# Projection chunks that accumulate onto the running sum in PSUM, filled and copied back by ScalarE, and group-norm sums added onto zeros

## The chip, the cores and the metric

The kernel runs on one core of one Trainium2 chip. The core has a matrix engine (TensorE, PE in the profile) that writes into PSUM, eight banks of 128 partitions x 512 floats, a vector engine (VectorE, DVE), a scalar engine (ScalarE, ACT), GpSimd (POOL), and DMA queues that SyncE (SP), ScalarE and GpSimd issue to. The metric is the device time of one execution in microseconds, as the median of several runs. Each engine works through its own list of instructions in the order of that list, and waits for the others by semaphores.

## The reference, cut to what matters

One block of a diffusion backbone in float32: adaLN-modulated RMSNorm, one input projection, attention beside a short gated convolution, group norm, output projection, gated MLP. The change touches the input projection and the group norm of the convolution's half:

```python
h_l = modulate(rms_norm(x, g_mix_norm[l]), sh_a, sc_a)            # 512 tokens x 2048
qa_l, kva_l, kr_l, cb_l, cc_l, ch_l = split_projection(h_l @ w_in[l])
...
conv_l = short_conv(cb_l, cc_l, ch_l, conv_w[l], conv_b[l])
x = x + gt_a * merge_heads(att_l, conv_l, g_mix_out[l], w_out[l])  # RMSNorm over groups of 128, then @ w_out
```

## The kernel before

Everything is kept transposed: a tile is 128 features x 512 tokens. The input projection has 31 such output tiles ("columns" below, the weights in `ORDER`), and its sum runs over 16 input tiles h0 to h15. Float32 accuracy is made from a high and a low part of both operands: `mm3` (line 200) issues three matmuls for each product, high x high (L202), high x low (L203), low x high (L204). So each piece of weights is first cast by ScalarE (`split`, L181, the high part) and then subtracted by VectorE (L182, the low part).

The sixteen inputs become ready one after another, because each needs two rows of adaLN weights, which VectorE multiplies out (L256, and for the context L667) from `ada` tiles that stream in over SyncE's queue through four buffers. The projection is therefore cut into three chunks of the sum: `KCH = [2, 4, 10]` inputs. Chunk 0 (h0, h1) is written out earlier in the function. Chunks 1 and 2 run in the loop at lines 829 to 875. Each begins with six columns at once (`first_banks`, tiles `pf`, weights `wf` from loads `rf`), and goes on with the other 25 columns one by one: a bank from `bank`, tile `pp`, `n` calls of `mm3` (n = 4 in chunk 1, 10 in chunk 2), then `evac`. Weights come as `rw` loads: in chunk 1 four columns to a load on GpSimd's queue, in chunk 2 one column to a load of 640 KB on SyncE's queue. There are two raw buffers, and one is free again when VectorE has made its last low part; the cast weights (`w_0h`, `w_4h`, `w_8h` and the l's) have about five buffers.

`evac` (line 673) keeps a running sum `acc[m]` in SBUF. In chunk 0 ScalarE copies the bank there. In chunks 1 and 2 VectorE adds the bank to it (L678). After chunk 2 it starts what follows for the column: `low_rank`, `rope_key`, or, for the columns of the convolution, `conv` (L604 to L611), `gn_sum` and `gn_apply`. `gn_sum` (line 390) squares a finished tile on ScalarE (L392), sums it over the 128 features with four matmuls against a column of ones (L396), each into its own column of a bank, and lets VectorE copy the four numbers out (L397).

`bank` (line 120) deals banks in turn: four single ones (tag "s") and two double ones (tag "b"), whose halves go to two successive dealings, though both halves are one tile. So the columns 13 and 14 share the tile that the trace calls `pp_13`, 17 and 18 share `pp_17`, 21 and 22 share `pp_21`, and so on.

The order of the instructions on each engine is not written out by hand here, but where `keep` pins it: the framework's scheduler lays the program out on a timeline of its own and fixes the order by that. Loads through `fetch_to` are pinned to the program's order until chunk 1's first columns are done (`ordered`, L852), and are free after it.

Of the kernel before, what the change touches and what calls it, by code (L numbers as in the profile page):

```python
# [13 lines left out]
ALU = mybir.AluOpType  # L14
# [3 lines left out]
P = 128  # L18
# [57 lines left out]
def block_kernel(ctx, tc, xt, ctxt, ctxn, c, c_ctx, w_ada, small, w_in, w_inc, w_q, w_kv, w_out,  # L76
# [3 lines left out]
    V, A, G_, PE, SP = nc.vector, nc.scalar, nc.gpsimd, nc.tensor, nc.sync  # L80
# [19 lines left out]
    def t2(shape, dt, name):  # L100
        return act.tile(shape, dt, tag="t2", bufs=NT2, name=name)

    def tmp(shape, dt, name):
        return tp.tile(shape, dt, tag="tmp", bufs=5, name=name)
# [7 lines left out]
    def sml(nm):  # L112
        return one_bank[0](nm) if one_bank[0] else pp.tile([P, 512], F32, tag="s", bufs=4, name=nm)

    def big(nm):
        return pp.tile([P, 1024], F32, tag="b", bufs=2, name=nm)
# [3 lines left out]
    def bank(nm):  # L120

        if turn[1] is not None:
            h, turn[1] = turn[1], None
            return h
        i = turn[0] = (turn[0] + 1) % 6
        if i % 3:
            return sml(nm)
        b = big(nm)
        turn[1] = b[:, 512:]
        return b[:, :512]  # L130

    def first_banks(nm, n):
        turn[:] = (5 if n == 6 else 0), None
        r = [sml(f"{nm}{g}") for g in range(4)]
        for g in range(4, n, 2):
            b = big(f"{nm}{g}")
            r += [b[:, :512], b[:, 512:]]
        return r
# [55 lines left out]
    def part(w, i, n=1):  # L194
        return tuple(z[:, i * P:(i + n) * P] for z in w)
# [4 lines left out]
    def mm3(ps, w, x, first, last, on_top=False):  # L200
        with tc.issue_after(behind.pop()) if behind else ExitStack():
            PE.matmul(ps, w[0], x[0], start=first, stop=False, skip_group_check=on_top)  # L202
        PE.matmul(ps, w[0], x[1], start=False, stop=False, skip_group_check=on_top)  # L203
        PE.matmul(ps, w[1], x[0], start=False, stop=last, skip_group_check=on_top)  # L204
# [26 lines left out]
    ident, ones = io[:, :P], io[:, P:]  # L231
# [158 lines left out]
    def gn_sum(t, o):  # L390
        sq = tmp([P, T], F32, f"gq{t}")
        A.activation(sq, o, AF.Square)  # L392
        yield
        ps = sml(f"gp{t}")
        for g in range(4):
            PE.matmul(ps[:, g:g + 1], sq[:, g * P:(g + 1) * P], ones[:, 0:1], start=True, stop=True)  # L396
        V.tensor_copy(out=gn[:, 4 * t:4 * t + 4], in_=ps[:, :4])  # L397
        yield

    def gn_apply(t, o):  # L400
        pb = sml(f"gb{t}")
        spread(pb, gn[:, 4 * t:4 * t + 4])
        V.scalar_tensor_tensor(out=o, in0=o, scalar=s("g_out", 8 + t), in1=pb, op0=ALU.mult, op1=ALU.mult)
        yield
# [9 lines left out]
    def low_rank(tiles, g, width, nm, res):  # L414
        sq = None
        for t in tiles:
            sq = add_squares(sq, t, width, nm)
            yield
        r = tmp([P, T], F32, nm + "r")
        rms([sq], len(tiles) * P, width, r)  # L420
        yield
        for i, t in enumerate(tiles):
            V.scalar_tensor_tensor(out=t, in0=t, scalar=s(g, i), in1=r[:, :width], op0=ALU.mult, op1=ALU.mult)
            res.append(hilo(t, T, nm + f"{i}") if width == T else hilo_pair(t, nm + f"{i}"))
            yield
# [3 lines left out]
    with ExitStack() as pa:  # L429
# [19 lines left out]
        hl = {}  # L449
# [107 lines left out]
        for j in range(NK):  # L557
# [6 lines left out]
            if j in (2, 4, 6, 8):  # L564
                g = j // 2 - 1
# [24 lines left out]
        n = GCH[0] * P  # L590
# [5 lines left out]
        def rope_key():  # L596
            rope(acc[6], bank("kr"), "kr")
            yield
            krl.extend(hilo(acc[6], T, "krl"))
            yield  # L600

        def conv(t):
            cc, ch, cb = (acc[7 + 3 * t + i] for i in range(3))
            V.tensor_tensor(out=cc, in0=cc, in1=ch, op=ALU.mult)  # L604
            u = ch
            yield
            A.activation(u, cc, AF.Identity, bias=s("cb", t), scale=s("cw", 8 + t))
            V.scalar_tensor_tensor(out=u[:, 1:], in0=cc[:, :T - 1], scalar=s("cw", t), in1=u[:, 1:], op0=ALU.mult, op1=ALU.add)
            V.scalar_tensor_tensor(out=u[:, :T - 1], in0=cc[:, 1:], scalar=s("cw", 16 + t), in1=u[:, :T - 1], op0=ALU.mult, op1=ALU.add)
            yield  # L610
            V.tensor_tensor(out=cb, in0=cb, in1=u, op=ALU.mult)  # L611
            mixc.append(cb)
            yield
# [56 lines left out]
        cm = ctx_mods()  # L670
        acc = {}

        def evac(ci, m, ps):
            if ci == 0:
                acc[m] = t2([P, T], F32, f"acc{m}")
                A.copy(out=acc[m], in_=ps)
                return
            V.tensor_tensor(out=acc[m], in0=acc[m], in1=ps, op=ALU.add)  # L678
            if ci < 2:
                return  # L680
            if m == 3:
                bg.appendleft(low_rank([acc[i] for i in range(4)], "g_q", T, "qa", qan))
            elif m == 5:
                bg.appendleft(low_rank([acc[i] for i in (4, 5)], "g_kv", T, "kl", kvl))
            elif m == 6:
                bg.appendleft(rope_key())
            elif m >= 9 and m % 3 == 0:
                q = bg if m < 27 else post
                q.append(conv((m - 9) // 3))
                q.append(gn_sum((m - 9) // 3, acc[m]))  # L690
                late_bg.append(gn_apply((m - 9) // 3, acc[m]))
# [57 lines left out]
        for i, (ci, bs, off, size, b) in enumerate(stream):  # L749
# [25 lines left out]
            n = KCH[ci]  # L775
            hi, lo = ready[i]
            for z in ([0, 2, 1] if i in (0, 2) else [None]):
                for e, (q, m) in enumerate(bs):
                    assert K0[ci] + q in done
                    w, x = part((hi, lo), e), hl[K0[ci] + q]  # L780
# [48 lines left out]
        for ci, k0, n in ((1, K0[1], KCH[1]), (2, K0[2], KCH[2])):  # L829

            pss = first_banks(f"pf{ci}", G)
            if ci == 2:
                bg.append(ctx_stats())
            for q in range(n):
                if ci == 2:
                    if q in (2, 4):
                        modulate(13 + q // 2)
                    next(cm)
                    pump(1)
                if q % 2 == 0:  # L840
                    if ci == 1:
                        w = first_rows[q // 2]
                    else:
                        raw = load(w_in[:, off:off + 2 * G * P], 2 * G * P, f"rf{ci}{q}")
                        w = blocks(raw, 2 * G, f"wf{ci}{q}")
                    off += 2 * G * P
                for g in range(G):
                    mm3(pss[g], w[q % 2 * G + g], hl[k0 + q], q == 0, q == n - 1)
            for g in range(G):
                evac(ci, ORDER[g], pss[g])  # L850
            if ci == 1:
                ordered[0] = False  # L852
            per, step = max(1, 2048 // (n * P)), max(1, 4 // n)
            for i, m in enumerate(ORDER[G:]):
                if i % per == 0:
                    k = min(per, len(ORDER) - G - i) * n
                    raw = load(w_in[:, off:off + k * P], k * P, f"rw{ci}_{m}", G_ if ci == 1 else None)
                    off += k * P
                if i % step == 0:
                    ws = blocks(raw, min(step, len(ORDER) - G - i) * n, f"w{ci}_{m}", i % per * n)  # L860
                w = ws[i % step * n:(i % step + 1) * n]
                ps = bank(f"pp{ci}_{m}")
                for kk in range(n):
                    mm3(ps, w[kk], hl[k0 + kk], kk == 0, kk == n - 1)
                evac(ci, m, ps)
                for f, j in todo.get((ci, i), []):
                    f(j)
                if ci == 2:
                    for q in range(2 if i % 4 == 0 else 1):
                        next(cm, None)  # L870
                    if 20 <= i <= 22:
                        late_both((lambda t: ada_tiles(p_sb, 4, w_ada[t], f"ae{t}")) if i < 22 else None)
                    if i >= 5 and i % 2 == 1 and (i - 5) // 2 < CTX_EARLY:
                        bg.append(ctx_prep((i - 5) // 2))
                    pump(2)
# [30 lines left out]
    with ExitStack() as pb:  # L906
# [284 lines left out]
        for k in range(OUT_EARLY):  # L1191
            if k % 2 == 0:
                w = row_weights(w_out_first, k, "of", raw=out_raw[k])
# [82 lines left out]
    for k in range(OUT_EARLY, NK):  # L1276
        if k % 2 == 0:
            w = row_weights(w_out_first, k, "of")
# [8 lines left out]
    for h in range(2):  # L1287
        for i in range(2):
            ps = whole(raws[i], mix, f"o{NK - 2 + i}{h}", pso[i], HS[h], ld=ada_spare)
# [196 lines left out]
    for k in range(EARLY, NK):  # L1486
        w = nxt
# [165 lines left out]
    for h in range(2):  # L1653
        ps = [bank8(f"d{h}{i}") for i in range(8)]
        for k in range(STD):
# [3 lines left out]
            w = split4(fetched.popleft(), 1024, f"dw{h}{k}")  # L1659
# [313 lines left out]
```

## Time and profile before

| | us |
|---|---|
| median of 3 runs | 2125.85 (2124.03 to 2126.39) |
| profiled execution, its own time | 2129.29 |
| its span, first to last instruction | 2127.5 |
| mean granted clock of TensorE | 0.994 |

The profiled execution is 3.44 us above the median of the other runs. In the rows of the trace, "a <- b" is output and input; a row of a timeline gives start, duration, engine, line, operation and tiles, and in brackets how long the engine sat idle before it and for whom. A row of the windows gives, for a stretch from the span's start, the busy time of each engine and the number of its instructions in brackets, then the granted clock of TensorE, the mean busy share of the 16 DMA engines, and GB/s. Matmuls overlap, so the duration of one (0.39 us) is longer than the distance from one to the next. In this trace chunk 1 runs from about 72 to 157 us, chunk 2's first six columns from 157 to 209, and its 25 other columns from there to about 400.

### The profile page before, as it was taken

To read this page: it belongs to the slowest core of one execution; us is meant where nothing else is said; L and a number is where in the kernel's file an instruction comes from. 1 tells how busy PE (TensorE), PEld (TensorE's weight loads), DVE (VectorE), ACT (ScalarE), POOL (GpSimd) and SP (SyncE) were. 2 spreads that over 40 slices of the span, in tenths; PEclk is the share of its full clock that TensorE was granted. 3 is DMA by queue.
4 is the path that set the end of the run, shared out by engine and by line. 5 is a ranking of instruction groups with operands and counts; after the bars stand their busy time and mean duration, and the time that the engine had idled before them with its cause. 6 is when DMAs were issued, how large, how long until landed. Compare 5 with 4: busy or idle time off the path is not lost.

```text
span 2127.5 us, 35260 instructions
## 1 busy us (share of the span) xinstructions
PE 2088.2 (98%) x13303; PEld 1880.9 (88%) x13303; DVE 1821.0 (86%) x2952; ACT 1049.5 (49%) x1715; POOL 127.7 (6%) x161
## 2 busy tenths in 40 slices
PE   8999999999999999999999999999999999999997
PEld 6777778889888889999999999999999889999997
DVE  7898987878887888898999999999999659887887
ACT  6534233555552337555555655655555333333445
POOL 0000000000010000111000000000000000000000
PEclk9999999999999999999999999999999999999999
DMA  9799877435658975577888878888888989878684
GB/s 343 278 323 325 298 263 236 138 129 198 208 191 325 335 284 164 154 223 212 226 232 238 235 220 239 240 228 230 240 229 231 366 304 309 246 230 240 195 237 136
DMA packets 165885, 514.78 MB, mean 242 GB/s; under 512 B 18641, under 2 KB 22993, under 8 KB 155985
## 3 DMA queue, kind: packets, MB, share of 16 engines
q1 hardware_dynamic: 127024, 407.90, 56.7%
q0 software_dynamic: 19312, 70.40, 15.7%
q10 hardware_dynamic: 19378, 34.23, 4.2%
q8 instruction: 104, 1.70, 0.3%
q14 instruction: 67, 0.55, 0.1%
HBM read 465.26 MB, written 46.14 MB: 240 GB/s over the span
## 4 chain that ended last, share of the span: by engine, by line
PE 88%; DVE 5%; DMA 3%; issue 2%; ACT 2%; POOL 0%; DVEq 0%; SPq 0%; ACTq 0%; POOLq 0%
PE pp L202 3%; PE pp L204 3%; PE pp L203 3%; PE o L202 1%; PE o L204 1%; PE o L203 1%; PE d L202 1%; PE d L203 1%; PE d L204 1%; PE uf L202 1%; PE uf L203 1%; PE uf L204 1%; PE of L202 1%; PE of L204 1%; PE of L203 1%
## 5 line engine op out<-in xcount | busy, mean ns | idle before, releaser
L1445 POOL DMA_DIRECT2D u_s<-in_w_up x80 | 68.4, 855 | 682.5 <-DMA u_s<-in_w_up 402.9
L285 DVE SCALAR_TENSOR_TENSOR ada<-ada,sv 128x2048 f32<-128x2048 f32 x33 | 75.5, 2289 | 16.0 <-DMA ada<-in_w_ada 15.6
L181 ACT CAST w_0h<-rw 128x512 fp32r<-128x512 f32 x50 | 30.5, 620 | 99.2 <-DMA rw<-in_w_in 49.8
L667 DVE SCALAR_TENSOR_TENSOR ada<-ada,svc 128x1024 f32<-128x1024 f32 x64 | 76.1, 1217 | 1.9 <-DMA ada<-in_w_ada 1.9
L1566 DVE TENSOR_TENSOR u<-u,u_s 128x1024 f32<-128x1024 f32 x40 | 48.7, 1218 | 4.0 <-DMA u_s<-in_w_up 4.0
L281 DVE SCALAR_TENSOR_TENSOR ra<-ra,sv 128x1024 f32<-128x1024 f32 x42 | 49.8, 1216 | 0.0
L256 DVE SCALAR_TENSOR_TENSOR ada<-ada,sv 128x1024 f32<-128x1024 f32 x40 | 48.3, 1213 | 0.8 <-DMA ada<-in_w_ada 0.8
L1567 DVE TENSOR_TENSOR u<-u,u 128x1024 f32<-128x1024 f32 x40 | 48.6, 1216 | 0.0
L182 DVE TENSOR_TENSOR w_0l<-rw,w_0h 128x512 fp32r<-128x512 f32 x50 | 33.9, 682 | 15.4 <-ACT w_0h L181 15.2
L1071 POOL TENSOR_TENSOR gr<-gr,half 128x8 f32<-128x8 f32 x4 | 11.2, 2809 | 488.1 <-DVE gr L1070 458.1
L1365 DVE TENSOR_TENSOR tp<-a,tp 128x256 fp32r<-128x256 f32 x90 | 37.5, 416 | 2.9 <-ACT tp L1364 2.9
L1364 ACT CAST tp<-a 128x256 fp32r<-128x256 f32 x90 | 35.7, 403 | 6.6 <-DMA yl6h<-y_d 3.7
L1042 ACT CAST pth<-t 128x384 fp32r<-128x384 f32 x64 | 28.6, 486 | 18.0 <-PE t L1039 17.9
L1043 DVE TENSOR_TENSOR ptl<-t,pth 128x384 fp32r<-128x384 f32 x64 | 33.1, 548 | 3.9 <-ACT pth L1042 3.9
L1328 ACT ACTIVATE g<-g 128x512 f32<-128x512 f32 x43 | 27.2, 634 | 18.0 <-DVE g L1322 17.7
L678 DVE TENSOR_TENSOR acc<-acc,pp 128x512 f32<-128x512 f32 x50 | 33.8, 677 | 1.5 <-PE pp L204 1.5
L1021 DVE TENSOR_REDUCE mn<-s 128x1 f32<-128x768 f32 x32 | 30.3, 950 | 4.9 <-PE s L1010 4.9
L1320 ACT ACTIVATE g<-cg,sm 128x512 f32<-128x512 f32 x40 | 32.6, 815 | 0.0
L1320 ACT ACTIVATE a<-ca,sm 128x512 f32<-128x512 f32 x40 | 32.1, 802 | 0.0
L1024 ACT ACTIVATE p<-s,mn 128x768 f32<-128x768 f32 x32 | 29.3, 914 | 4.3 <-DVE mn L1021 4.1
L1321 DVE SCALAR_TENSOR_TENSOR g<-cg,sm,g 128x511 f32<-128x511 f32 x40 | 29.8, 745 | 0.0
L1321 DVE SCALAR_TENSOR_TENSOR a<-ca,sm,a 128x511 f32<-128x511 f32 x40 | 29.8, 745 | 0.0
(10435 smaller groups left out, 8966.4 us busy)
## 6 DMA issues: line engine op xcount, KB each, us to landing
ada<-in_w_ada SPq DMA_DIRECT2D x128, 512.0 KB, 5.9
u<-in_w_up SPq DMA_DIRECT2D x120, 512.0 KB, 9.2
w<-t_d SPq DMA_DIRECT2D x161, 256.0 KB, 5.3
u_s<-in_w_up SPq DMA_DIRECT2D x80, 512.0 KB, 4.0
u_s<-in_w_up POOLq DMA_DIRECT2D x80, 512.0 KB, 9.7
ada<-in_w_ada SPq DMA_DIRECT2D x33, 1024.0 KB, 6.2
t_d<-tp ACTq DMA_DIRECT2D x126, 256.0 KB, 6.0
v<-in_w_dnw SPq DMA_DIRECT2D x72, 384.0 KB, 5.7
```

What stands on the lines that cost most here:

```text
L202: PE.matmul(ps, w[0], x[0], start=first, stop=False, skip_group_check=on_top)
L203: PE.matmul(ps, w[0], x[1], start=False, stop=False, skip_group_check=on_top)
L204: PE.matmul(ps, w[1], x[0], start=False, stop=last, skip_group_check=on_top)
L256: ins = V.scalar_tensor_tensor(out=r, in0=r, scalar=1.0, in1=vec[:, i * 1024:(i + 1) * 1024], op0=ALU.mult, op1=ALU.mult, accum_out=col[:, ...
L281: keep(V.scalar_tensor_tensor(out=halves[i], in0=halves[i], scalar=1.0, in1=svs[i], op0=ALU.mult, op1=ALU.mult, accum_out=lc[:, t % 4:t % ...
L285: keep(V.scalar_tensor_tensor(out=r, in0=r, scalar=1.0, in1=sv, op0=ALU.mult, op1=ALU.mult, accum_out=mod[:, t:t + 1]))
L667: keep(V.scalar_tensor_tensor(out=raw[q], in0=raw[q], scalar=1.0, in1=svc[:, q * 1024:(q + 1) * 1024], op0=ALU.mult, op1=ALU.mult, accum_o ...
L1320: A.activation(u, src, AF.Identity, bias=s("fb", m), scale=s("fw", 86 + m))
L1321: V.scalar_tensor_tensor(out=u[:, 1:], in0=src[:, :T - 1], scalar=s("fw", m), in1=u[:, 1:], op0=ALU.mult, op1=ALU.add)
L1445: G_.dma_start(r[-1], src[more], accum_op=ALU.add)
L1566: V.tensor_tensor(out=a11, in0=a11, in1=s1, op=ALU.add)
L1567: V.tensor_tensor(out=a12, in0=a12, in1=a11, op=ALU.add)
```

## The change

In chunks 1 and 2 the 25 columns that go one by one no longer start on an empty bank. ScalarE first copies the running sum into the bank (the new line 868), all matmuls then add onto what stands there (`start` is False for all of them), and after the last one ScalarE copies the whole sum back to `acc[m]` (the new line 680). VectorE's add is gone for these 50 banks; it stays for the six first columns of each chunk, twelve banks, where `evac` is called as before. In `gn_sum` VectorE writes zeros to the four numbers first (new line 395), and the four matmuls add onto them.

```diff
@@ gn_sum
         ps = sml(f"gp{t}")
+        V.tensor_scalar(ps[:, :4], ones[:, :4], scalar1=0.0, scalar2=None, op0=ALU.mult)
         for g in range(4):
-            PE.matmul(ps[:, g:g + 1], sq[:, g * P:(g + 1) * P], ones[:, 0:1], start=True, stop=True)
+            PE.matmul(ps[:, g:g + 1], sq[:, g * P:(g + 1) * P], ones[:, 0:1], start=False, stop=True, skip_group_check=True)
@@ evac
-        def evac(ci, m, ps):
+        def evac(ci, m, ps, whole_sum=False):
...
-            V.tensor_tensor(out=acc[m], in0=acc[m], in1=ps, op=ALU.add)
+            if whole_sum:
+                A.copy(out=acc[m], in_=ps)
+            else:
+                V.tensor_tensor(out=acc[m], in0=acc[m], in1=ps, op=ALU.add)
@@ chunks 1 and 2, the columns that go one by one
                 ps = bank(f"pp{ci}_{m}")
+                if ci:
+                    A.copy(out=ps, in_=acc[m])
                 for kk in range(n):
-                    mm3(ps, w[kk], hl[k0 + kk], kk == 0, kk == n - 1)
-                evac(ci, m, ps)
+                    mm3(ps, w[kk], hl[k0 + kk], kk == 0 and ci == 0, kk == n - 1, on_top=ci > 0)
+                evac(ci, m, ps, True)
```

The scheduler lays out the whole program anew, so more moves than these lines say. TensorE, at the start of chunk 2's single columns, in the kernel before and then in the changed one (`pf` are the first six columns; `w_13_8h` is the last of the three pieces of column 13's weights; the columns 13 and 14 are the halves of the tile `pp_13`):

```order
L204 MATMUL pf_1558<-h15h,wf_8l 128x512
L203 MATMUL pp_13_1924<-h15l,w_13_8h 128x512
L204 MATMUL pp_13_1924<-h15h,w_13_8l 128x512
L324 MATMUL rcb<-io,rsc 128x128 x2
L202 MATMUL pp_15_2040<-h6h,w_15_0h 128x512
L203 MATMUL pp_15_2040<-h6l,w_15_0h 128x512
L202 MATMUL pp_13_1924<-h6h,w_14_0h 128x512
```

```order
L202 MATMUL pp_13_1949<-h15h,w_13_8h 128x512
L203 MATMUL pp_13_1949<-h15l,w_13_8h 128x512
L204 MATMUL pp_13_1949<-h15h,w_13_8l 128x512
L202 MATMUL pp_15_2067<-h6h,w_15_0h 128x512
L203 MATMUL pp_15_2067<-h6l,w_15_0h 128x512
L202 MATMUL pp_13_1949<-h6h,w_14_0h 128x512
```

Before, the end of the first six columns ran between the matmuls of column 13; now column 13 runs as one piece behind them. In both, two matmuls of column 15 stand between column 13 and column 14.

ScalarE at the same place, before and then after (`rw_15` is the load of column 15's weights; L868 is the fill of a bank, L680 the copy back):

```order
L181 CAST w_14_0h<-rw_14_1972 128x512
L181 CAST w_15_0h<-rw_15_2026 128x512
L181 CAST w_15_4h<-rw_15_2026 128x512
L639 COPY rc<-rcb 128x256
L607 ACTIVATE acc_403<-acc_401,sm 128x512
L181 CAST w_15_8h<-rw_15_2026 128x256
```

```order
L868 COPY pp_16_2128<-acc_470 128x512
L640 COPY rc<-rcb 128x256
L181 CAST w_14_8h<-rw_14_1998 128x256
L868 COPY pp_17_2185<-acc_500 128x512
L181 CAST w_15_0h<-rw_15_2053 128x512
L181 CAST w_15_4h<-rw_15_2053 128x512
L680 COPY acc_435<-pp_13_1949 128x512
L868 COPY pp_13_1949<-acc_437 128x512
```

Most fills stand columns ahead of their matmuls; the copy of column 13 and the fill of column 14 stand together, behind two casts of column 15's weights.

SyncE's queue of loads around the same columns, before and then after (all `ada` loads have 512 KB; `cg` is a context tile):

```order
L150 DMA rw_15_2026<-in_w_in 128x1280
L150 DMA ada_1710<-in_w_ada 128x1024
L150 DMA ada_1712<-in_w_ada 128x1024
L150 DMA ada_1752<-in_w_ada 128x1024
L150 DMA ada_1754<-in_w_ada 128x1024
L150 DMA ada_1780<-in_w_ada 128x1024
L621 DMA cg_2549<-in_ctxt 128x512
L150 DMA rw_16_2085<-in_w_in 128x1280
```

```order
L150 DMA rw_14_1998<-in_w_in 128x1280
L150 DMA ada_1735<-in_w_ada 128x1024
L150 DMA ada_1737<-in_w_ada 128x1024
L150 DMA ada_1777<-in_w_ada 128x1024
L150 DMA ada_1779<-in_w_ada 128x1024
L150 DMA rw_15_2053<-in_w_in 128x1280
L150 DMA ada_1805<-in_w_ada 128x1024
L622 DMA cg_2589<-in_ctxt 128x512
```

Four `ada` loads that followed column 15's weights now go ahead of them. From column 18's weights on the loads stand where they stood, give or take three places.

## The prediction

> **What bounds the kernel now.** I read the page first, then the waits of TensorE, then windows around each wait, then the rows at their edges.
>
> ```profile
> span 2127.5 us, 35260 instructions
> ...
> PE 2088.2 (98%) x13303; PEld 1880.9 (88%) x13303; DVE 1821.0 (86%) x2952; ACT 1049.5 (49%) x1715; POOL 127.7 (6%) x161
> ...
> PE 88%; DVE 5%; DMA 3%; issue 2%; ACT 2%; POOL 0%; DVEq 0%; SPq 0%; ACTq 0%; POOLq 0%
> ```
>
> TensorE is busy for 98% of the span and carries 88% of the chain that ended last. The change keeps the number of its matmuls, so the time can move only through TensorE's waits and through its clock. The sum below is made against the profiled execution, 2129.29 us, and is carried over to the median, which is 3.44 lower. The next rows are windows over the stages: TensorE's busy time with its matmuls in brackets, weight loads, VectorE, ScalarE, GpSimd, then clock, DMA share and GB/s.
>
> ```profile
> 80.00:157.00 77.00, 76.53 (x329) 61.74 (x329) 76.14 (x148) 27.75 (x42) 2.65 (x5) 1.00 0.88 314
> 157.00:209.00 52.00, 51.29 (x221) 41.30 (x220) 42.38 (x84) 22.30 (x38) 0.00 (x0) 1.00 0.93 332
> 209.00:410.00 201.00, 190.58 (x830) 153.40 (x829) 169.97 (x329) 68.78 (x133) 0.00 (x0) 0.97 0.71 241
> 210.00:220.00 10.00, 5.75 (x16) 4.55 (x16) 10.00 (x18) 1.42 (x4) 0.00 (x0) 0.66 0.75 258
> 280.00:290.00 10.00, 8.87 (x26) 6.68 (x27) 9.80 (x21) 3.45 (x8) 0.00 (x0) 0.66 0.87 275
> 110.00:133.00 23.00, 23.00 (x100) 18.65 (x100) 23.00 (x44) 9.54 (x13) 1.05 (x2) 1.00 0.98 364
> 200.00:260.00 60.00, 54.06 (x230) 43.27 (x230) 56.03 (x109) 18.64 (x34) 0.00 (x0) 0.94 0.88 307
> ```
>
> In chunk 1 (80 to 157) VectorE is full, yet TensorE misses only 0.5 us: taking 25 adds away there gains nothing by itself. What can be gained lies in chunk 2's single columns, 209 to 410, where TensorE is idle for 10.4 us and its clock is 0.97. These are the waits there, in total, with their number and the longest; and then the rows at their ends.
>
> ```profile
> PE pp L202 <- ACT w_0h L181: 4.4, 3, 2.5
> PE pp L202 <- DVE acc L678: 4.3, 1, 4.3
> ...
> 213.53 0.68 DVE L678 TENSOR_TENSOR acc<-acc,pp 128x512 f32<-128x512 f32 x1
> 214.13 0.68 DVE L182 TENSOR_TENSOR w_0l<-rw,w_0h 128x512 fp32r<-128x512 f32 x1
> 214.26 0.79 PE L202 MATMUL pp<-h6h,w_0h 128*128 128x512 f32 x1 [4.25 <-DVE acc L678]
> ...
> 247.33 0.51 PE L202 MATMUL pp<-h6h,w_0h 128*128 128x512 f32 x1 [1.41 <-ACT w_0h L181]
> 248.35 0.50 PE L204 MATMUL pp<-h6h,w_0l 128*128 128x512 f32 x1 [0.28 <-DVE w_0l L182]
> ...
> 280.28 0.50 PE L202 MATMUL pp<-h6h,w_0h 128*128 128x512 f32 x1 [2.48 <-ACT w_0h L181]
> 281.95 0.80 PE L204 MATMUL pp<-h6h,w_0l 128*128 128x512 f32 x1 [0.85 <-DVE w_0l L182]
> ```
>
> Three places, which I call A, C and B. **A**: column 14 waits 4.25 us because it shares a bank tile with column 13, whose add comes late on VectorE. **C** (1.41 + 0.28) and **B** (2.48 + 0.85): the first product of columns 19 and 23 waits for its weights. At full clock 100 matmuls take 23.00 us, 0.23 each. Behind A 16 matmuls took 5.75 us instead of 3.7, behind B 26 took 8.87 instead of 6.0, both windows at a clock of 0.66: 2.1 and 2.9 us lost beside the idle time. So A costs 6.3, B 6.2, C 1.7 us; 14.2 together is the most that can be won.
>
> The Trainium skill ("TensorE: Matmul & The Clock Gate", section "HAM oscillation — how this bites in real kernels") says that the clock falls for TensorE gaps over about 3.4 us. By that rule B's gap would cost no clock and only 11.3 us could be won; the windows have the low clock behind a gap of 2.48 with 0.85 soon after, and the measurement decides.
>
> **The change, part by part.**
>
> ```profile
> L678 DVE TENSOR_TENSOR acc<-acc,pp 128x512 f32<-128x512 f32 x50 | 33.8, 677 | 1.5 <-PE pp L204 1.5
> ...
> L736 ACT COPY acc<-pp x23: 573/604/662, 45.0 to 72.4; 128x512 f32<-128x512 f32 x23
> ...
> L397 DVE COPY gn<-gp x8: 149/154/163, 237.3 to 428.1; 128x4 f32<-128x4 f32 x8
> ```
>
> *Fills and copies.* VectorE loses 50 adds. One lasts 0.68 but the next instruction starts 0.60 behind it (213.53, 214.13), so 30 us go. ScalarE gains 50 copies back and 50 fills. A copy out of a bank takes 0.60 (chunk 0's rows). A fill into a bank is not shown: between 0.57, the shortest of those copies, and 0.81, the longest ScalarE instruction on a tile of this size in chunk 2; I take 0.60, as it is the same operation and size. That is 30 us more in each chunk: ScalarE goes from 27.75 to 58 of 77 us, and from 68.8 to 99 of 201. It becomes no bound. Most fills stand columns ahead of their matmuls and cost TensorE nothing; without that lead each would cost 0.6.
>
> *Zeros.* Eight writes of 128x4, between the 0.15 of the small copy in these rows and the 0.68 of an add; I take 0.15, nearest in size, 1.2 us of VectorE, less than what it loses. In the program they stand columns ahead of their four matmuls, so TensorE does not wait; uncovered they would cost 8 x 0.15.
>
> *The pair at A.* Column 14 now waits for "copy 13, fill 14" on ScalarE, and the order puts this pair behind two casts of column 15's weights. Those casts wait for a load that now stands behind four more `ada` loads.
>
> ```profile
> 198.29 0.33 SPq L150 DMA_DIRECT2D rw<-in_w_in  x1
> 198.82 9.73 SPq L150 DMA_DIRECT2D ada<-in_w_ada  x5
> ...
> DMA to landing us min/median/max: 4.1/6.5/8.1
> ```
>
> The first row is that load's issue, the second the five `ada` issues behind it, 1.95 us each, the third the flight of chunk 2's weights at this place. At the old pace it is issued at 198.3 + 4 x 1.95 = 206.1, lands at 212.6, and after two casts (0.62 each) and the pair (1.2) column 14 starts at 215.0, 0.8 later than now. If the queue runs ahead (VectorE has 15 us less to do in chunk 1, and it is VectorE that the loads wait for, below), only the pair itself is left: 1.2 plus about 0.2 for the handing over, less two matmuls of column 15 in between (0.46), 0.9; then A gains 5.4. So A lies between +0.8 and -5.4.
>
> The Trainium skill ("PSUM — Partial Sum Buffer", section "Engine vs sequencer instructions") has ScalarE's queue as strictly first in, first out. By it the pair cannot pass a cast that waits for its load, which gives the +0.8; if it could pass, A would gain 5.4 in either case.
>
> *The pace of the loads at C and B.* Each load of weights is issued when VectorE has made the last low part from the buffer that it goes to:
>
> ```profile
> 234.01 0.39 ACT L181 CAST w_8h<-rw 128x256 fp32r<-128x256 f32 x1
> 239.83 0.41 DVE L182 TENSOR_TENSOR w_8l<-rw,w_8h 128x256 fp32r<-128x256 f32 x1
> 240.26 0.33 SPq L150 DMA_DIRECT2D rw<-in_w_in  x1
> 246.66 0.62 ACT L181 CAST w_0h<-rw 128x512 fp32r<-128x512 f32 x1 [4.35 <-DMA rw<-in_w_in]
> ...
> L678 DVE TENSOR_TENSOR acc<-acc,pp x4: 672/676/679, 213.5 to 242.0; 128x512 f32<-128x512 f32 x4
> ...
> L678 DVE TENSOR_TENSOR acc<-acc,pp x7: 672/677/680, 213.5 to 268.6; 128x512 f32<-128x512 f32 x7
> ...
> SPq L150 <- DVE ada L667: 103.4, 53, 6.2
> ```
>
> ScalarE had cast the buffer's last piece by 234.4; VectorE came to it 5.4 us later, and at once the load went out, which C waited for. So VectorE sets the pace, and SyncE's queue waits most for VectorE's products (103.4 us over 80 to 410). Three adds stand ahead of C's load (the fourth starts at 242.0), seven ahead of B's: the loads come 3 x 0.60 = 1.8 and 7 x 0.60 = 4.2 us earlier.
>
> *The sum.* If A gains 5.4: TensorE comes to C 5.4 earlier, the load only 1.8, so it waits 1.7 + 3.6 = 5.3, longer than at A, and loses some 2.5 by the clock (between 2.1 and 2.9): it leaves C 0.7 late. At B it would wait 2.48 - 0.7 = 1.8; the load is 4.2 earlier; B is gone with its clock, 6.2 - 0.7 = 5.5 us won. If A loses 0.8: C's 1.7 goes wholly (the load is 1.8 earlier), 0.9 won; B would be a wait of 2.48 + 0.9 = 3.4, still under 4.2, so it goes too: 7.1 won. The middle is 6.3. The other two pairs, columns 17 and 18 and columns 21 and 22, have two matmuls and the four small group-norm matmuls between them, 0.1 to 0.2 us over each (bounds: nothing, and 0.9 as at A): minus 0.4. **Forecast: -5.9**, 2123.4 on the profiled execution, **2120.0** as a median.
>
> **The rivals.**
>
> *All three waits go.* The loads run ahead by more than the adds tell, since the order also moves products: -14.2 + 0.9 + 0.4 = -12.9, about 2113, at best 2111.7. Against it: it needs loads over 5 us earlier at C, where three adds give 1.8.
>
> *The transfers set the pace.* From 200 to 260 the DMA engines are busy for 0.88 of the time with 307 GB/s. If the loads for C and B land when they did, those two end when they did; what A gains becomes idle time at C. The sum is 0 to +1.8 for the pairs: 2125.9 to 2127.7. Against it: 0.98 and 364 GB/s were reached at 110 to 133.
>
> *Slower: the loads of chunk 2's first six columns are late.* In the new order of SyncE's queue the first of them stands three `ada` loads further back.
>
> ```profile
> 121.00 24.58 SPq L150 DMA_DIRECT2D ada<-in_w_ada  x10
> 147.05 0.33 SPq L150 DMA_DIRECT2D rf<-in_w_in  x1
> ...
> 153.34 0.62 ACT L181 CAST wf_0h<-rf 128x512 fp32r<-128x512 f32 x1 [4.01 <-DMA rf<-in_w_in]
> ...
> 156.57 0.39 PE L202 MATMUL pf<-h6h,wf_0h 128*128 128x512 f32 x1
> ```
>
> At 2.46 us for each `ada` it goes out at 154.4 instead of 147.05, lands 6.3 later at 160.7, and its first cast ends at 161.3. TensorE used it first at 156.57, at a pinch it could be needed at 158.6: idle for 2.7 to 4.7, and 2.1 to 2.9 by the clock, 5 to 7.6 us. With the forecast's gain this ends near no change; with transfers that set the pace it is 2131 to 2135. It decides from an issue after about 151 (158 less 6.3 and 0.6). Against it: 133 to 157 was not full on the DMA engines (0.88 is the mean with 0.98 in it), and VectorE, which the `ada` loads wait for, is relieved there.
>
> *The change does not do what it says*: twelve adds stay on VectorE, and the adds of the six `pf` banks are the very ones that stand ahead of column 13's add at A. If VectorE were not relieved where it matters, the time would be as in the rival of the transfers, and I count it there.
>
> **How the numbers follow.** Forecast 0.40, all gone 0.10, transfers 0.25, slower 0.25. A measurement of this kernel can tell about 0.2%, 4.25 us, from no change: faster is below 2121.6, slower above 2130.1. The forecast's two branches run from 7.5 to 5.1 won, 2118.3 to 2120.8, and up to 1.5 more for pairs at their upper bound; I count 0.32 of its 0.40 as faster. Faster 0.10 + 0.32 = 0.42; same 0.08 + 0.22 = 0.30; slower 0.25 + 0.03 = 0.28. The range takes in most of "all gone" below (2112) and the slower rival but its end above (2134).
>
> **What the changed kernel's profile would show.** VectorE's adds on banks: 12 left, all on `pf`. ScalarE's copies: 100 more, near 0.60. At A: column 14's wait, ended by ScalarE's fill instead of VectorE's add, and the issue of column 15's weights near 206 or well before. At C and B: the issue times of the loads against VectorE's last low part; right if B's wait and the low clock at 280 to 290 are gone, with clock 1.00 there. Slower is right if `pf` shows a wait for weights near 157 to 161 and the clock falls there. The forecast is wrong if fills or copies last much over 0.8, if a load waits for a fill, or if a wait of the old size stands at B with its load issued right behind VectorE's low part.

## The result, and the profile after

| | before | changed |
|---|---|---|
| median of 6 runs each | 2124.49 us | 2111.57 us (2109.67 to 2116.09) |
| ratio | | 0.9942, interval 0.9929 to 0.9955 |
| span of the profiled execution | 2127.5 us | 2109.6 us |

The change wins 12.9 us by the medians, 12.3 by the ratio. Set on the 2125.85 us that the prediction was made against, the ratio gives 2113.5. The forecast was 2120.0, 5.9 us won, in a range from 2112 to 2134: the sign held, the gain is about double the forecast, and the time lies at the range's lower end, where the rival "all three waits go" stands with 2113. The page's first lines after:

```profile
span 2109.6 us, 35335 instructions
...
PE 2079.0 (99%) x13303; PEld 1873.8 (89%) x13303; DVE 1792.2 (85%) x2910; ACT 1100.9 (52%) x1815; POOL 127.7 (6%) x161
```

The new copies and fills, VectorE's adds that are left, and the zeros, each as the answer for its line of the program gives it (number, shortest, median and longest in ns, first and last start):

```profile
L680 ACT COPY acc<-pp x50: 563/580/602, 95.5 to 394.6; 128x512 f32<-128x512 f32 x50
...
L868 ACT COPY pp<-acc x50: 576/591/611, 74.6 to 382.0; 128x512 f32<-128x512 f32 x50
...
L682 DVE TENSOR_TENSOR acc<-acc,pf x12: 676/678/689, 88.4 to 206.0; 128x512 f32<-128x512 f32 x12
...
L395 DVE TENSOR_SCALAR gp<-io x8: 151/156/159, 207.2 to 401.1; 128x4 f32<-128x4 f32 x8
```

Copies, fills and zeros cost what was taken for them. The windows over the same stages:

```profile
80.00:157.00 77.00, 76.61 (x330) 61.80 (x329) 69.06 (x136) 51.60 (x90) 2.97 (x6) 1.00 0.90 336
157.00:209.00 52.00, 52.00 (x227) 42.15 (x226) 43.22 (x83) 26.80 (x47) 0.00 (x0) 1.00 0.94 337
209.00:410.00 201.00, 199.39 (x941) 163.86 (x940) 162.51 (x322) 101.07 (x194) 0.00 (x0) 1.00 0.70 246
```

TensorE's waits from 72 to 410 us (total, number, longest):

```profile
PE pp L202 <- ACT pp L868: 1.6, 3, 1.2
PE pp L204 <- DVE w_0l L182: 0.4, 1, 0.4
```

From 209 to 410 TensorE is idle for 1.6 us instead of 10.4, at a clock of 1.00 instead of 0.97. A is a wait of 1.17 us for the fill, without the low clock behind it; C and B are gone. The first attention matmul of head 0 starts at 422.68 us; before, at 437.01. These are 14.3 us, although this execution came 1.6 us late into chunk 0's thirteenth column (66.35 against 64.75). The rest of the program adds little: 14.5 us at the first matmul on `d` (1648.21 against 1662.76). That the spans lie 17.9 apart comes from the last 450 us, where both run the same instructions, and this execution of before was 4.8 us above the median of the six. In the next section, one execution of the change with chunk 1's adds back took 2661 us at a clock of 0.71, and its ratio is taken without it.

### The profile page after: what moved, and what is told of

Same layout as the page of the kernel before. It is cut to its first block, busy times and chain, and to the rows that moved or that the text cites. A ratio compares the mean times of both kernels' runs of the same rounds, so it can differ in the third digit from the quotient of the medians.

```text
span 2109.6 us, 35335 instructions
## 1 busy us (share of the span) xinstructions
PE 2079.0 (99%) x13303; PEld 1873.8 (89%) x13303; DVE 1792.2 (85%) x2910; ACT 1100.9 (52%) x1815; POOL 127.7 (6%) x161
## 4 chain that ended last, share of the span: by engine, by line
PE 88%; DVE 4%; DMA 3%; issue 2%; ACT 2%; POOL 0%; DVEq 0%; SPq 0%; POOLq 0%; ACTq 0%
PE pp L202 4%; PE pp L204 4%; PE pp L203 4%; PE o L203 1%; PE o L204 1%; PE o L202 1%; PE d L202 1%; PE d L203 1%; PE d L204 1%; PE uf L202 1%; PE uf L203 1%; PE uf L204 1%; PE of L202 1%; PE of L203 1%; PE of L204 1%
## 5 line engine op out<-in xcount | busy, mean ns | idle before, releaser
L668 DVE SCALAR_TENSOR_TENSOR ada<-ada,svc 128x1024 f32<-128x1024 f32 x64 | 77.0, 1218 | 1.2 <-DMA ada<-in_w_ada 1.2
L1334 ACT ACTIVATE g<-g 128x512 f32<-128x512 f32 x43 | 27.3, 634 | 18.2 <-DVE g L1328 17.9
L680 ACT COPY acc<-pp 128x512 f32<-128x512 f32 x50 | 29.0, 580 | 5.4 <-PE pp L204 5.4
L868 ACT COPY pp<-acc 128x512 f32<-128x512 f32 x50 | 29.2, 589 | 1.7 <-DVE acc L682 0.9
```

Of the source, the lines that this page charges most:

```text
L668: keep(V.scalar_tensor_tensor(out=raw[q], in0=raw[q], scalar=1.0, in1=svc[:, q * 1024:(q + 1) * 1024], op0=ALU.mult, op1=ALU.mult, accum_o ...
```

## The experiments

All ratios are to runs of the kernel before on the same chip. The last column is the number of context products (L667 before, L668 in the changed kernel, 64 in all) that VectorE had begun by 209 and by 240 us of the profiled span; it measures how far ahead its stream of work is.

| kernel | median, us | ratio (interval) | products |
|---|---|---|---|
| before | 2124.5 | 1 | 9, 22 |
| the change | 2111.6 | 0.9942 (0.9929 to 0.9955) | 11, 26 |
| fills alone, no zeros | 2111.9 | 0.9937 (0.9924 to 0.9950) | 12, 27 |
| zeros alone | 2127.4 | 1.0010 (1.0001 to 1.0020) | 9, 23 |
| chunk 1 alone | 2118.1 | 0.9963 (0.9950 to 0.9976) | 12, 26 |
| chunk 1 alone, its adds back | 2119.4 | 0.9975 (0.9966 to 0.9985) | 11, 24 |
| chunk 2 alone | 2119.3 | 0.9973 (0.9961 to 0.9984) | 9, 23 |
| column 13 alone | 2122.5 | 0.9985 (0.9976 to 0.9994) | 9, 22 |
| the change, chunk 1's adds back | 2114.1 | 0.9955 (0.9941 to 0.9968) | 10, 24 |
| the change, chunk 2's adds back | 2120.6 | 0.9980 (0.9968 to 0.9991) | 12, 26 |
| fills by VectorE | 2126.9 | 1.0013 (1.0003 to 1.0022) | 9, 22 |
| all columns filled | 2115.9 | 0.9962 (0.9950 to 0.9975) | 13, 28 |
| also chunk 2's first six | 2110.5 | 0.9939 (0.9927 to 0.9952) | 13, 28 |
| both halves together | 2108.1 | 0.9930 (0.9917 to 0.9944) | 12, 26 |

**Which part carries it.** Four kernels with one part each.

```diff
 # fills alone: gn_sum as before
-        V.tensor_scalar(ps[:, :4], ones[:, :4], scalar1=0.0, scalar2=None, op0=ALU.mult)
-            PE.matmul(ps[:, g:g + 1], ..., start=False, stop=True, skip_group_check=True)
+            PE.matmul(ps[:, g:g + 1], ..., start=True, stop=True)
 # chunk 1 alone, chunk 2 alone, zeros alone
+                top = ci == 1        # ci == 2; False
-                if ci:
+                if top:
                     A.copy(out=ps, in_=acc[m])
...
```

> The fills and copies back of both chunks, without the zeros in the group-norm sums. If the fills carry the change, 10 to 14 us are won, as with the whole change (12.9 by the medians). If the zeros carry part of it (no wait of a group-norm matmul for VectorE stood in the profile before), less than 10. In the profile: no idle time of TensorE over 2 us between 200 and 300 us.

> Fills and copies back in chunk 1 only, 25 adds fewer there; chunk 2 adds as before. By the step of the prediction that says adds in chunk 1 gain nothing by themselves: within 2 us of the kernel before, A, C and B with their idle times of 4.3, 1.7 and 3.3 us. Rival, the work that moves ahead: the relieved VectorE makes adaLN products earlier, so that fewer are left in chunk 2; then the load of column 19's weights goes out more than 3 us earlier than at 240.3 and at least 5 us are won.

> Fills and copies back in chunk 2 only; loads and products up to column 13 stand as before. By the prediction's steps: A shrinks from 4.25 to about 1 us, the loads of columns 19 and 23 come 1.8 and 4.2 us earlier, 5 to 7 us are won and C still waits, longer than before. Rival, the work that moves ahead in chunk 1 is needed: under 3 us. Rival, the wait at A alone set the pace of what follows: 11 us or more, and the load of column 19 over 5 us earlier.

> Only the zeros that VectorE writes ahead of the group-norm sums, with the adds of before. Eight small writes of VectorE of some 0.15 us: 0 to 1.2 us slower, not to be told from no change. Rival: TensorE waits for a write of zeros that stands late on the full VectorE, once or more often: 2 us or more slower, with such a wait in the list of TensorE's waits.

The fills alone give the whole gain. The zeros alone cost 2.1 us by the ratio, with an interval that begins at 0.2; that is more than the 1.2 expected, which the interval still holds, and no wait for a write of zeros stands among TensorE's waits; the fills without them are not measurably faster than the change. (The kernels with chunk 2's fills and without zeros, here and below but for column 13 alone, lose the running sum of some columns, as the last section tells; that changes values, not the instructions that run.) The two chunks add up: chunk 1 alone is 7.6 and chunk 2 alone 6.4 us below the kernel before, which had a median of 2125.7 on their chip; that is 14.0 together beside 12.9. Chunk 1, which was to give nothing, gives at least as much as chunk 2 (their intervals overlap). The windows from 80 to 157 and 157 to 209 us of its profile:

```profile
80.00:157.00 77.00, 76.85 (x332) 62.00 (x331) 69.05 (x138) 51.80 (x90) 2.65 (x5) 1.00 0.91 339
157.00:209.00 52.00, 52.00 (x226) 42.16 (x225) 43.27 (x82) 23.98 (x41) 0.00 (x0) 1.00 0.92 331
```

Its waits at A and C, from the timeline:

```profile
212.10 0.50 PE L204 MATMUL pp<-h6h,w_0l 128*128 128x512 f32 x1 [2.46 <-DVE w_0l L182]
245.16 0.50 PE L202 MATMUL pp<-h6h,w_0h 128*128 128x512 f32 x1 [2.04 <-ACT w_0h L181]
```

VectorE is 69.05 + 43.27 us busy instead of 76.14 + 42.38, only 6.2 less although 15 us of adds are gone: it did 8.8 us of other work that used to come later, and enters chunk 2's single columns with 12 context products begun instead of 9. At A TensorE now waits for the low part of column 15's weights, and the wait is shorter also because 14 matmuls of column 15 stand ahead of column 14 here, not two; C is still there and B is gone.

Chunk 2 alone is the kernel that the prediction's sum describes, and the number came true, 6.4 us for 5.9: products and loads up to column 13 stand as before (9 products by 209, the load of column 15's weights at 198.76 against 198.29). Its parts did not all come true. Its A was 0.80 and 0.55 us. The longer wait at C did not come; one of 1.86 and 0.63 us fell on column 16 instead. And B was not gone: 1.77 us were left there, at 277.88, with a low clock behind them. So the agreement is in part luck.

**Is it VectorE's time?** The freed time is put back as an add that nobody waits for; one bank of fifty is treated alone; the fills go to VectorE.

```diff
 # the change, chunk 2's adds back (chunk 1's: ci == 1)
             if whole_sum:
                 A.copy(out=acc[m], in_=ps)
+                if ci == 2:
...
+                    V.tensor_tensor(out=spare["idle"], in0=acc[m], in1=acc[m], op=ALU.add)
 # column 13 alone
+                top = ci == 2 and i == 0
 # fills by VectorE
-                    A.copy(out=ps, in_=acc[m])
+                    V.tensor_copy(out=ps, in_=acc[m])
```

> The changed kernel, and for each of the 25 single columns of chunk 2 VectorE also adds the finished sum to itself into a tile that nobody reads: its work in chunk 2 is back, but no bank and no later step waits for it. If the relief of VectorE's time in chunk 2 carries chunk 2's share (6.4 us in the run with chunk 2 alone), about 5 to 7 us are lost against the changed kernel, near 2118, with waits for weights' low parts again between 225 and 300 us. If what matters there is that bank and sum no longer wait for VectorE, the time stays within 2 us of the changed kernel's 2111.6.

> Chunk 1 alone filled, and VectorE's 25 adds of chunk 1 put back in the same way, into a tile that nobody reads. SyncE's loads keep the order of the run with chunk 1 alone nearly place by place (70 adaLN loads ahead of column 13's weights, before it were 66). If the time freed on VectorE carries chunk 1's share (7.6 us), it goes: 2123 to 2127. If it is the order of loads and products, it stays: 2117 to 2120. If banks that are free sooner carry it, it stays as well, but then A's wait is that of the run with chunk 1 alone, 2.5 us.

> Only column 13 of chunk 2 is filled and copied back by ScalarE, one bank of fifty; column 14 keeps its add and its empty bank. The wait at A falls from 4.25 us to under 1.5 and the low clock behind it goes, some 5 us. If the loads of columns 19 and 23 follow VectorE's work, they come at most 1 us earlier, and C and B give those 5 us back: 0 to 2 us won. If TensorE's stop at A holds up all that follows, weights' buffers and loads with it, 5 us or more are won and column 19's load goes out 4 us earlier than at 240.3.

> All fifty fills by VectorE instead of ScalarE, copies back still by ScalarE, no zeros. A fill is a copy of the size of the add, so VectorE's work is back to nearly the old amount, but ahead of the matmuls instead of behind them. If the freed time of VectorE carries the change: most of it is lost, 2120 to 2126, and VectorE is over 95% busy from 80 to 157 us. If the end of a column (add, then bank free) carries it: 2111 to 2115.

With chunk 2's adds back 8.1 of the 12.3 us go by the ratios, whose intervals do not meet, though neither a bank nor a sum waits for VectorE: in chunk 2 it is VectorE's time that counts. Two of its waits:

```profile
240.81 0.80 PE L202 MATMUL pp<-h6h,w_0h 128*128 128x512 f32 x1 [1.47 <-ACT w_0h L181]
...
334.11 0.50 PE L202 MATMUL pp<-h6h,w_0h 128*128 128x512 f32 x1 [3.16 <-ACT w_0h L181]
```

The window behind the first of them, with the clock at 0.66:

```profile
240.00:250.00 10.00, 8.78 (x25) 6.55 (x26) 9.58 (x21) 3.18 (x6) 0.00 (x0) 0.66 0.89 294
```

Both are waits for a cast that itself waited for its load: the same kind as C and B. Fills by VectorE say the same from the other side: the end of a column is as in the change, VectorE is 76.45 of 77 us busy in chunk 1, and nothing is won, 2.0 us lost.

Column 13 alone takes A away (0.27 us left), and the trace shows where its 6.3 us go: to column 16's weights, whose load comes no earlier (issued at 211.01, before at 210.03).

```profile
211.28 0.50 PE L202 MATMUL pp<-h6h,w_0h 128*128 128x512 f32 x1 [0.27 <-ACT acc L679]
227.62 0.75 PE L202 MATMUL pp<-h6h,w_0h 128*128 128x512 f32 x1 [2.60 <-ACT w_0h L181]
230.73 0.79 PE L204 MATMUL pp<-h6h,w_0l 128*128 128x512 f32 x1 [1.93 <-DVE w_0l L182]
```

Won were 2.4 us, and column 19's load went out at 240.13, before at 240.26. So the stop at A did not set the pace of the rest; the rival of that name falls.

Chunk 1's adds, put back, cost less than chunk 1's share: of 0.0037 in the ratio 0.0025 stay (7.9 and 5.3 us), with intervals that overlap. The window from 157 to 209 us, and those of the put-back adds that started in it:

```profile
157.00:209.00 52.00, 52.00 (x226) 41.79 (x224) 47.91 (x94) 22.75 (x40) 0.00 (x0) 1.00 0.93 325
...
L683 DVE TENSOR_TENSOR idle_sum<-acc x12: 672/685/693, 161.4 to 200.9; 128x512 f32<-128x512 f32 x12
```

VectorE has all its adds and is nevertheless two products ahead by 209 us. But the adds did not come back where they had been. Before, 23 of chunk 1's 25 adds started by 157 us, in the full stretch; here, where nobody waits for them, only 13 did, and 12 ran behind it, where VectorE used to idle. They account for its 47.91 us there instead of 42.38. So about half of the time freed in chunk 1 stayed free, and the order stayed as well: four more `ada` loads ahead of column 13's weights, 70 against 66, as in chunk 1 alone. This run does not tell the freed time from the order of loads.

**What is left.** Three kernels build on the change, one puts chunk 1's adds back into it.

```diff
 # all columns (chunk 2's first six alone: for ci == 2 only)
             pss = first_banks(f"pf{ci}", G)
+            for g in range(G):
+                A.copy(out=pss[g], in_=acc[ORDER[g]])
...
-                    mm3(pss[g], w[q % 2 * G + g], hl[k0 + q], q == 0, q == n - 1)
+                    mm3(pss[g], w[q % 2 * G + g], hl[k0 + q], False, q == n - 1, on_top=True)
...
-                evac(ci, ORDER[g], pss[g])
+                evac(ci, ORDER[g], pss[g], True)
 # both halves together, chunk 2
+                if ci == 2 and held:
+                    ps = held.pop(0)
...
+                    if ci == 2 and turn[1] is not None and i + 1 < len(ORDER) - G:
+                        held.append(bank(f"pp{ci}_{ORDER[G + i + 1]}"))
+                        A.copy(out=held[0], in_=acc[ORDER[G + i + 1]])
...
+                if held:
+                    owed.append((m, ps))
+                else:
+                    while owed:
+                        evac(ci, *owed.pop(), True)
+                    evac(ci, m, ps, True)
```

> The changed kernel with the six first columns of each chunk filled and copied back by ScalarE too: the last twelve adds leave VectorE, six of them from the stretch 206 to 213 us ahead of column 13's end. If VectorE's time in chunk 2 still bounded the changed kernel, 1 to 3 us below 2111.6. TensorE waits for weights nowhere any more from 80 to 410 us in the changed kernel, only 1.2 us for a fill, so by that reading there is nothing left to win: within 1.5 us. Rival: the six fills in a row (3.6 us of ScalarE) stand ahead of the first matmuls of a chunk: 2 us or more slower, with a wait for a fill near 75 or 157 us.

> The same for chunk 2's first six columns alone, six adds fewer between 200 and 213 us. Nothing left to win: within 1.5 us of the changed kernel. Rival: fills in a row at 157 us hold up TensorE, 1 us or more slower.

> The changed kernel, with both halves of a double bank filled at once ahead of the first one's matmuls in chunk 2, and both copied back behind the second one's. Column 14 waits neither for the copy of column 13 nor for its own fill: the idle time of 1.17 us at A goes, about 1 us won, 2110 to 2111.5. If the late copy back holds up the convolution's group instead, a new wait for it stands between 215 and 300 us and the time is 1 us or more longer.

> The changed kernel with VectorE's 25 adds of chunk 1 put back into a tile that nobody reads (the run before it of this kind put back chunk 2's and lost 9 us). If the time freed on VectorE in chunk 1 carries chunk 1's share, 5 to 8 us are lost, 2117 to 2120, and fewer than 11 context products are done by 209 us. If the order of loads and products carries it (70 adaLN loads ahead of column 13's weights here, as in the changed kernel), the time stays within 2 us of 2111.6. In between, 2 to 5 us, both do.

Both halves together is the best of all, 2108.1 us; its interval overlaps with the change's, but the trace shows the step: A's wait is gone, and TensorE waits for nothing from 209 to 410 us.

```profile
209.00:410.00 201.00, 201.00 (x968) 166.64 (x967) 162.85 (x323) 100.04 (x195) 0.00 (x0) 1.00 0.70 245
```

Six adds fewer in chunk 2 change nothing (2110.5), as was read from the change's profile: VectorE's time there is no bound any more. All twelve fewer are slower than the change, 2115.9, by intervals that just overlap. The rival with the fills in a row did not come; another did, at columns 21 and 22. ScalarE's timeline, then TensorE's:

```profile
270.56 0.62 ACT L181 CAST w_4h<-rw 128x512 fp32r<-128x512 f32 x1
271.08 0.58 ACT L680 COPY acc<-pp 128x512 f32<-128x512 f32 x1
271.69 0.59 ACT L870 COPY pp<-acc 128x512 f32<-128x512 f32 x1
```

```profile
272.33 0.80 PE L202 MATMUL pp<-h6h,w_0h 128*128 128x512 f32 x1 [1.52 <-ACT pp L870]
```

The window behind that wait:

```profile
272.00:282.00 10.00, 9.67 (x29) 7.70 (x30) 7.80 (x17) 2.37 (x6) 0.00 (x0) 0.67 0.84 292
```

This is the pair behind casts that the prediction priced at A: late by 1.52 us, and with the low clock (0.67) behind it some 3 us more. In the changed kernel the pair cost 1.17 us at A and 0.22 at columns 21 and 22, and no clock.

With chunk 1's adds back the change loses 0.0013 of its ratio, 2.8 us, with 10 and 24 products; chunk 1 alone lost 0.0012, 2.6 us, by the same edit. Here too 13 of the 25 adds ran behind 157 us, and neither difference is clear of its intervals. How chunk 1's share divides between the time freed on VectorE and the order of loads stays open.

## Why the prediction was right and wrong

- *What bounds the kernel*: right. From chunk 0's thirteenth column to the attention 15.9 us were won (14.3, and the 1.6 of the late entry). TensorE's idle time from 72 to 410 us fell by 9.6 us and the low clock's 5.0 are gone, 14.6 of them.
- *"Taking 25 adds away there gains nothing by itself"*: **this step failed.** It is true of TensorE inside chunk 1, and chunk 1 alone won 7.6 us in chunk 2. The prediction let chunk 1's relief count only at A, for the load of column 15's weights, and put it at nothing for C and B. The rows for it were quoted: VectorE full up to 157 us, idle for 9.6 of the 52 us after that, and full again at A. Work that can be made earlier flows from a full stretch into the idle one ahead of the next full one, if the loads for it are there.
- *The pace of the loads*: the mechanism was right, VectorE's last low part sends them off, and chunk 2's adds put back brought such waits again. Its size was wrong, and for the same reason: "1.8 and 4.2 us earlier" counted chunk 2's adds only. In the changed kernel:

```profile
198.65 0.38 SPq L150 DMA_DIRECT2D rw<-in_w_in  x1
...
232.45 0.39 SPq L150 DMA_DIRECT2D rw<-in_w_in  x1
...
261.93 0.38 SPq L150 DMA_DIRECT2D rw<-in_w_in  x1
```

  These are the issues of the weights of columns 15, 19 and 23. Column 19's went out 7.8 us earlier (240.26 before), column 23's 11.3 (273.22). The same two issues in chunk 2 alone:

```profile
237.40 0.38 SPq L150 DMA_DIRECT2D rw<-in_w_in  x1
...
268.45 0.33 SPq L150 DMA_DIRECT2D rw<-in_w_in  x1
```

  And in chunk 1 alone:

```profile
237.25 0.37 SPq L150 DMA_DIRECT2D rw<-in_w_in  x1
...
265.90 0.33 SPq L150 DMA_DIRECT2D rw<-in_w_in  x1
```

  Chunk 2 alone brings 2.9 and 4.8 us, not far from the 1.8 and 4.2; chunk 1 alone brings 3.0 and 7.3, which the sum did not have. With 7.8 and 11.3 in the sum, and A's 5.4, TensorE comes to C 5.4 + 1.7 earlier at most, under 7.8, and to B 7.1 + 2.5, under 11.3: both waits go, and 5.4 + 1.7 + 6.2 - 0.4 = 12.9, the rival's sum.
- *The pair at A*: 1.17 us against 0.9, and the branch was the good one. The load of column 15's weights, four `ada` loads further back, went out at 198.65, not at 206.1; the "old pace" was not kept. ScalarE's rows show the pair where it was expected, behind two casts:

```profile
208.50 0.62 ACT L181 CAST w_0h<-rw 128x512 fp32r<-128x512 f32 x1 [1.18 <-PE pp L203]
209.90 0.62 ACT L181 CAST w_4h<-rw 128x512 fp32r<-128x512 f32 x1 [0.78 <-PE pp L203]
210.43 0.58 ACT L680 COPY acc<-pp 128x512 f32<-128x512 f32 x1
211.04 0.59 ACT L868 COPY pp<-acc 128x512 f32<-128x512 f32 x1
```

  The casts waited for buffers that TensorE frees, not for the load.
- *The rivals*: "all three waits go" had the time, 2113, and a chance of 0.10; it was held unlikely because it needs loads over 5 us earlier at C, and they came 7.8 us earlier. Transfers did not set the pace: the DMA engines were busy for 0.91 of the time from 209 to 260 and 0.95 from 260 to 310, and the loads came earlier all the same. The slower rival's load, three `ada` loads back, went out at 148.04, not 154.4, and TensorE waited for nothing there.
- *Forecast*: as said of chunk 2 alone, it describes half of the change. That the time still lies in the range is owed to the rival, whose 2113 the range took in, and not to the forecast.

## What to carry to other kernels

An engine that is full in one stage, has room in the next and is late in the third is one bound, not three: relief in the first stage moves its later work forward, if the loads' order lets it. Before counting an off-path relief as nothing, look whether the engine idles between here and the next wait that it causes. Where two columns share a bank tile, fill both halves at once and copy both back at the end, so that no copy and fill stand between two runs of matmuls; the wait went here, and the time gained lies within the intervals.

## What the runs showed of the hardware

The low clock does not follow from the length of one gap. It fell at a gap of 1.47 us (0.66, chunk 2's adds back: 0.50 from 240.7 to 247.5 us, so it was low already when a second gap, of 0.40 us, came) and behind 0.67 and 1.52 (0.67, all columns), but not behind 2.04 at 245.16 in chunk 1 alone, nor behind 1.86 and 0.63 in chunk 2 alone, where it did fall behind 1.77 at 277.88. The window of chunk 1 alone:

```profile
243.00:253.00 10.00, 7.96 (x34) 6.09 (x34) 9.17 (x19) 3.31 (x6) 0.00 (x0) 1.00 0.91 326
```

Those of chunk 2 alone:

```profile
225.00:235.00 10.00, 7.51 (x35) 5.61 (x34) 10.00 (x20) 3.78 (x7) 0.00 (x0) 1.00 0.98 367
276.00:286.00 10.00, 8.22 (x29) 6.54 (x29) 9.83 (x23) 3.71 (x9) 0.00 (x0) 0.83 0.95 332
```

The clock is at 1.00 in the first two rows and at 0.83 in the third. The bound of 3.4 us that the Trainium skill names for gaps ("TensorE: Matmul & The Clock Gate", section "HAM oscillation — how this bites in real kernels") did not hold here as a safe one: 1.47 and 1.77 us were enough. What decides it these runs do not show.

The zeros in the group-norm sums are there for the fills. Without them the four small matmuls begin their sums afresh, and kernels with fills in chunk 2 then lost running sums of later columns: the relative error of the output was 0.89 (fills alone), 0.78 (chunk 2 alone) and 0.77 (fills by VectorE). The Trainium skill ("PSUM — Partial Sum Buffer", section "The four PSUM rules") says that a matmul which starts a sum clears the written-marks of its whole bank, and that the next matmul that adds onto an unmarked place overwrites it, whatever ScalarE or VectorE has put there; this agrees with the three kernels. The first of them differs from the change by nothing but the zeros and how those four matmuls start.
